# The squares of x added on VectorE, and the gate columns of group C brought forward in both layers

## The chip, the cores and the metric

The kernel runs on one core of one Trainium2 chip. The metric is the device time of one execution in microseconds. TensorE (PE) does the matrix multiplications, and its weight loads are listed apart as PEld; VectorE is DVE, ScalarE is ACT, GpSimd is POOL, and SyncE is SP, which here only issues transfers. Each engine executes its own queue in order and waits there for whatever its next instruction needs.

## The reference

Two layers work on 640 tokens of width 2048 (128 tokens of a prompt, 512 latent tokens). In each layer the normalised and modulated input goes through one combined projection, whose columns belong to three groups of heads; the three results go side by side through an output projection and are added to the input.

```python
shift, scale, gate = adaln(cvec, w_ada, b_ada)
h = rms_norm(x, norm_g) * (1.0 + scale) + shift
aq, ak, av, ag, bq, bff, bfb, bi, bg, cu, cv, cg = split_proj(h @ w_in)
q, k, v = qkv_heads(aq, ak, av, qg, kg, rope)
a_out = attend(q, k, v) * jax.nn.silu(ag)                       # A: attention, width 1024
b_out, s_f, s_b = hgrn_mixer(bq, bff, bfb, bi, bg, ...)          # B: gated recurrence, 4 heads, width 512
c_out = sgu_mixer(cu, cv, cg, lng, lnb, ws, bs)                  # C: cu * s(layer_norm(cv)) * silu(cg), width 512
y = jnp.concatenate([a_out, b_out, c_out], axis=-1) @ w_out
return x + gate * y, k, v, s_f, s_b
```

The modulation (shift, scale, gate) is a product of two vectors, one for prompt tokens and one for latent tokens, with a matrix of 2048 x 6144 per layer (w_ada).

## The kernel before, in words

*Projections.* The tokens lie as NT = 5 tiles of 128, the width as KT = 16 steps of 128. Each product in fp32 is made of three matmuls: weights are split into wh (ACT, L640) and wl (DVE, L641), activations into hh and hl, and hh·wh, hh·wl, hl·wh are summed. `rowmajor` gives 512 output columns with the tokens on the partitions: 240 matmuls (L652 to L654) into five PSUM banks "m". `colmajor` gives 128 output columns, columns on the partitions: 96 matmuls (L660) into two of those banks. There are five m banks in all, and three small ones, "s", for everything else.

*Work that rides along.* PE's long projections carry the rest of the layer in their gaps. A list `side` holds generators for the preparation of keys, the rotation of queries, the attention of one group and token tile (`attn`, whose rounds over key blocks end in the matmuls L953 to L955), the recurrence of a head (`hgrn`) and the mixing of group C (`sgu`). `tick` takes one step of the first of them, twice for each four steps of k in `colmajor` and about three times for each k in `rowmajor`; `flush` empties the list without further projection work in between. A second generator, the filler, computes the modulation that later stages need, in blocks of 512 columns: 16 steps, each of which loads 256 KB of w_ada and adds two products to a running sum on DVE (L302), then a step without work and one of closing matmuls on PE (L308 or L319). `fill` is called once at the end of each k group (15 times in a `rowmajor`, 4 times in a `colmajor`) and advances the filler by its rate: 1 in layer 0 (12 blocks, set before the projection AQ + 512) and 0.5 in layer 1 (4 blocks, set before AQ).

*Order.* The instructions of each engine are put in order by a scheduler when the kernel is built; what stands under `hi` goes ahead of other work that is ready. SP's queue issues nearly all loads of weights, in order; the ACT queue issues the small ones. Buffers come from pools: seven g of 128 x 640, five ev, five mg of 128 x 2560, four raw weights wr, three split weights, two for the filler's loads, and 16 each of hh and hl.

*Layer 0.* `setup` builds constants, among them the lower bounds of B's forget gates (L175 to L191). `first_round` loads x transposed, in four mg buffers; `first_norm` squares it on ACT, one k at a time, and sums over k and partitions with matmuls against a matrix of ones (L368), then takes the root (L370 to L372); then AK and the 128 columns of CU for head 0 are projected while the scale of the modulation comes in piece by piece (L240). `second_round` does AQ, `setup2` loads further constants, then come AQ + 512 and BI. CU 1 to 3 are projected and parked in DRAM (`cud`, by `cu_evac`), CU 0 is fetched back, multiplied by CG 0 and its SiLU, and parked again. Then come four heads of B with four `colmajor` each (BFF, BFB, BQ, BG), six of AG, the gates of A (`mul_evac`, whose last product POOL makes), a flush, CV with its layer norms, AG 6 and 7, a flush, in which `sgu` writes s into Cm. The four parked tiles are fetched and multiplied into Cm (L1354), then CG 1 to 3 are projected and multiplied into Cm as well, their last product on DVE. `split_mix` splits the 16 tiles of A, B and Cm into hh and hl (ACT, and L1229 on DVE or POOL), and `out_proj` multiplies by w_out in four `rowmajor`, whose results L1258 takes out of PSUM.

*Layer 1.* `begin_next` does the norm, AK, AQ, AQ + 512; then BI and the heads as above, seven AG, a flush, AG 7, CV, CU 0 and 1, a flush, CU 2 and 3 (multiplied into Cm straight from PSUM) and CG 0 to 3, all after the heads; `drain` finishes the filler, and the output projection writes the results.

The lines that say how a group is gated:

```python
s = self.ev() if gate else None
for hf, (o, n) in enumerate(HALF):                       # columns 0:384 and 384:640
    src = ps[hf][:, 0:n]
    if gate:
        nc.scalar.activation(s[:, o:o + n], src, AF.Exp, scale=-1.0)
    dv = dst[:, o // P:(o + n) // P, :]
    nc.vector.tensor_tensor(dv, dv, src.rearrange("p (t q) -> p t q", q=P), op=ALU.mult)   # L1208
if gate:
    self.sigma(s)                                        # min on DVE, Ln and Exp on ACT
    (eng or nc.gpsimd).tensor_tensor(dst, dst, s.rearrange(...), op=ALU.mult)              # L1211
```

Of the kernel before, what the change touches and what calls it, by code (L numbers as in the profile page):

```python
# [8 lines left out]
F32 = mybir.dt.float32  # L9
# [3 lines left out]
AF = mybir.ActivationFunctionType  # L13
ALU = mybir.AluOpType
# [4 lines left out]
P = 128  # L19
D = 2048  # L20
KT = D // P
# [3 lines left out]
NH = 4  # L25
# [3 lines left out]
HALF = ((0, 384), (384, 256))  # L29
AQ, AK, AV, AG = 0, 1024, 1280, 1536  # L30
BQ, BFF, BFB, BI, BG = 2560, 3072, 3584, 4096, 4608
CU, CV, CG = 5120, 5632, 6144
# [43 lines left out]
class Net:  # L76
# [57 lines left out]
    def setup(self):  # L134
        nc, I, C = self.nc, self.I, self.C
        cst = self.cst
        nc.scalar.preload_act_table_set("natural_log_exp_and_others")
        misc = cst.tile([P, 256], F32, name="misc")
        nc.sync.dma_start(misc, C["misc"])
        self.ident = misc[:, 0:128]  # L140
        self.m25 = misc[:, 192:217]
        self.dneg = misc[:, 224:244]
        self.sel = misc[:, 248:250]
        R = self.g(128)
        nc.scalar.dma_start(R[0:32], I["norm_g"].rearrange("l (a p) -> (l a) p", p=P))
        for l in range(2):
            nc.scalar.dma_start(R[32 + 32 * l:64 + 32 * l], I["b_ada"][l, 0:4096].rearrange("(a p) -> a p", p=P))
        nc.scalar.dma_start(R[96:112], I["hgrn_lb"].rearrange("l d (h p) -> (l d h) p", p=P))
        nc.scalar.dma_start(R[112:114], I["hgrn_norm_g"])
        CR = self.g(128)  # L150
        nc.sync.dma_start(CR[0:16], I["c_ctx"].rearrange("(a p) -> a p", p=P))
        nc.sync.dma_start(CR[16:32], I["c"][0].rearrange("(a p) -> a p", p=P))
        self.bias = cst.tile([P, 4], F32, name="bias")
        nc.vector.memset(self.bias[:, 0:1], EPS)
        nc.vector.memset(self.bias[:, 1:2], -0.5 * math.log(P))
        sg = self.g(128)
        nc.scalar.activation(sg[0:32], CR[0:32], AF.Exp, scale=-1.0)
        self.sigma(sg[0:32])
        nc.vector.tensor_tensor(sg[0:32], sg[0:32], CR[0:32], op=ALU.mult)
        self.sc = self.padded()  # L160
        self.shp = self.padded()
        self.s2 = cst.tile([P, KT, 2], F32, name="s2")
        self.ones = cst.tile([P, P], F32, name="ones")
        nc.vector.memset(self.ones, 1.0)
        b = self.bank()
        nc.tensor.transpose(b[:, 0:32], sg[0:32, :], self.ident[0:32, 0:32])
        for cd in range(2):
            nc.vector.tensor_copy(self.sc[:, :, cd], b[:, 16 * cd:16 * cd + 16])
            nc.vector.tensor_copy(self.s2[:, :, cd], b[:, 16 * cd:16 * cd + 16])
        b = self.bank()  # L170
        nc.tensor.transpose(b[:, 0:114], R[0:114, :], self.ident[0:114, 0:114])
        cols = cst.tile([P, 114], F32, name="cols")
        nc.vector.tensor_copy(cols, b[:, 0:114])
        self.cols = cols
        l0, l1 = cols[:, 96:104], cols[:, 104:112]  # L175
        lt = self.g(64).rearrange("p (a b) -> p a b", a=8)
        mx, e0, e1, sm_, p0, p1 = (lt[:, i] for i in range(6))
        nc.vector.tensor_tensor(mx, l0, l1, op=ALU.max)
        nc.vector.tensor_tensor(e0, l0, mx, op=ALU.subtract)
        nc.vector.tensor_tensor(e1, l1, mx, op=ALU.subtract)  # L180
        nc.scalar.activation(lt[:, 1:3], lt[:, 1:3], AF.Exp)
        nc.vector.tensor_tensor(sm_, e0, e1, op=ALU.add)
        nc.vector.reciprocal(sm_, sm_)
        nc.vector.tensor_tensor(p0, e0, sm_, op=ALU.mult)
        nc.vector.tensor_tensor(p1, e1, sm_, op=ALU.mult)
        self.lb = cst.tile([P, 2, 8], F32, name="lb")
        self.oml = cst.tile([P, 2, 8], F32, name="oml")
        nc.vector.tensor_tensor(self.lb[:, 0], p0, p0, op=ALU.subtract)
        nc.vector.tensor_tensor(self.lb[:, 1], p0, p1, op=ALU.add)
        nc.vector.tensor_tensor(self.lb[:, 1], self.lb[:, 1], p0, op=ALU.subtract)  # L190
        nc.vector.tensor_scalar(self.oml, self.lb, -1.0, 1.0, op0=ALU.mult, op1=ALU.add)  # L191
        self.gs = cst.tile([P, 2, KT, 2], F32, name="gs")
        self.sh = cst.tile([P, 2, KT, 2], F32, name="sh")

    def setup2(self):
        nc, I, C = self.nc, self.I, self.C
        cst = self.cst
        self.rope = cst.tile([P, 2, 4, 64], F32, name="rope")
        nc.scalar.dma_start(self.rope, C["rope"])
        self.scan_f = cst.tile([P, T], BF16, name="scan")  # L200
# [159 lines left out]
    def first_norm(self, xm):  # L360

        nc = self.nc
        b = [self.bank(), self.bank()]
        for k in range(KT):
            s = self.g()
            nc.scalar.activation(s, xm[k // 4][:, k % 4], AF.Square)
            for hf, (o, n) in enumerate(HALF):
                nc.tensor.matmul(b[hf][:, 0:n], lhsT=self.ones, rhs=s[:, o:o + n], start=k == 0, stop=k == KT - 1)  # L368
        r = self.g()
        for hf, (o, n) in enumerate(HALF):  # L370
            nc.scalar.activation(r[:, o:o + n], b[hf][:, 0:n], AF.Ln, bias=self.bias[:, 0:1], scale=1.0 / D)
        last = nc.scalar.activation(r, r, AF.Exp, scale=-0.5)  # L372
        return r, last.ins
# [938 lines left out]
    def layer(self, l):  # L1312
        W = self.I["w_in"][l]
        nc = self.nc
        self.hh, self.hl = [], []
        self.A, self.rq = {}, {}
        if l == 0:
            self.begin(W)
        else:
            self.begin_next(l, W)  # L1320
        self.side.append(self.q_rope(1))
        self.side += [self.attn(l, 1, t) for t in range(NT)]
        self.bi_evac(self.rowmajor(W, BI))
        if l == 0:
            for h in range(1, 4):
                self.cu_evac(h, self.colmajor(W, CU + h * P))
            u = self.g()
            nc.scalar.dma_start(u, self.cud[0])
            self.mul_evac(self.colmajor(W, CG), u.rearrange("p (t q) -> p t q", q=P), True, nc.vector)
            nc.scalar.dma_start(self.cud[0], u)  # L1330
        for h in range(NH):
            es = [self.z_evac(self.colmajor(W, c0 + h * P)) for c0 in (BFF, BFB)]
            q = self.q_gate(self.colmajor(W, BQ + h * P))
            if h == 0:
                self.flush()
            self.b_gate(l, h, self.colmajor(W, BG + h * P))
            self.side.append(self.hgrn(l, h, es, q))
        early = 6 if l == 0 else 7
        for h in range(early):
            self.mul_evac(self.colmajor(W, AG + h * P), self.av_view(h), True)  # L1340
        self.flush()
        if l > 0:
            self.mul_evac(self.colmajor(W, AG + 7 * P), self.av_view(7), True)
        self.sgu_evac(self.rowmajor(W, CV))
        self.side.append(self.sgu(l))
        if l == 0:
            ps = [self.colmajor(W, AG + h * P) for h in (6, 7)]
            self.flush()
            for h in (6, 7):
                self.mul_evac(ps[h - 6], self.av_view(h), True)  # L1350
            for h in range(4):
                u = self.g()
                nc.scalar.dma_start(u, self.cud[h])
                nc.vector.tensor_tensor(self.Cm[:, h], self.Cm[:, h], u, op=ALU.mult)  # L1354
        else:
            ps = [self.colmajor(W, CU + h * P) for h in range(2)]
            self.flush()
            for h in range(4):
                self.mul_evac(ps[h] if h < 2 else self.colmajor(W, CU + h * P), self.view(self.Cm, h), False)
        for h in range(1 - min(l, 1), 4):  # L1360
            self.mul_evac(self.colmajor(W, CG + h * P), self.view(self.Cm, h), True, nc.vector)
        if l > 0:
            self.drain()
        self.split_mix()
        self.out_proj(l)
        self.drain()

    def cu_evac(self, h, ps):
        nc = self.nc
        u = self.g()  # L1370
        with self.hi():
            nc.scalar.activation(u[:, 0:384], ps[0][:, 0:384], AF.Copy)
            nc.vector.tensor_copy(u[:, 384:640], ps[1][:, 0:256])
        nc.scalar.dma_start(self.cud[h], u)

    def run(self):
# [47 lines left out]
```

## Time and profile before

| what | value |
|---|---|
| median of three runs | 2344.2 us (2340.97 to 2345.61) |
| the profiled execution's own time | 2338.18 us |
| its span from the first to the last instruction | 2336.4 us |
| mean granted TensorE clock in it | 0.988 |
| busy: PE, PEld, DVE, ACT, POOL | 2261.4, 1968.0, 1424.3, 778.7, 293.9 us |
| read from and written to HBM | 280.38 and 13.73 MB, 126 GB/s over the span |

A row of a view by groups names the line, the engine, the operation, the output and the inputs by their pool names with shape and count, then busy time and mean; after a bar stands the idle time of the engine just before these instructions and what ended it. A row of the timeline has the start, the length, and in square brackets the wait just before. In a chain of waits, "PE s L1143 <- DVE g L1137: 7.0, 2, 6.1" says that PE's instruction at L1143 waited for DVE's at L1137, 7.0 us in all, twice, 6.1 us the longest. A row of the windows gives from and to, the length, the busy time and the number of instructions of PE, PEld, DVE, ACT and POOL, the granted clock (1.00 is full speed), the busy share of the DMA engines and what they moved in GB/s; where one line of one engine was asked for, its busy time alone stands in place of the five.

### The profile page before, as it was taken

The numbers are of one execution on the slowest core, as the hardware profiler recorded it, in microseconds if no ns is written. First come the engines' busy times: TensorE is split into PE (matmuls) and PEld (weight loads), VectorE is DVE, ScalarE is ACT, GpSimd is POOL, SyncE is SP. The second block draws the span as 40 slices with busy tenths as digits, with TensorE's granted clock in tenths as the row PEclk, the third lists the DMA queues.
The fourth block names the chain that finished last, engine by engine and source line by source line (L and its number), as shares of the span: only waits on it lengthen the run. The fifth ranks groups of instructions, "written<-read, shape, count | busy, mean of one in ns | idle before, by whom it ended". The sixth has DMA issues, their size and how long they took to land.

```text
span 2336.4 us, 34944 instructions
## 1 busy us (share of the span) xinstructions
PE 2261.4 (97%) x13308; PEld 1968.0 (84%) x13308; DVE 1424.3 (61%) x2612; ACT 778.7 (33%) x1605; POOL 293.9 (13%) x234
## 2 busy tenths in 40 slices
PE   7999999999999989989999999999999999999999
PEld 5766678899999888977787878799999998998887
DVE  3436987768887766666667455855875942434223
ACT  3323434343334322332224234344343332223111
POOL 0000111002122211011112010101222220101110
PEclk9999999999999999999999999999999999999999
DMA  9675632434433354355552221322332323324332
GB/s 321 218 254 191 209 117 83 148 95 120 126 117 104 111 163 144 111 192 171 173 170 91 77 68 47 115 68 72 111 94 76 114 90 92 103 75 149 106 106 84
DMA packets 264876, 296.41 MB, mean 127 GB/s; under 512 B 17378, under 2 KB 166772, under 8 KB 262916
## 3 DMA queue, kind: packets, MB, share of 16 engines
q1 hardware_dynamic: 254368, 271.27, 37.2%
q10 hardware_dynamic: 10340, 22.91, 3.2%
q8 instruction: 104, 1.70, 0.3%
q14 instruction: 64, 0.52, 0.1%
HBM read 280.38 MB, written 13.73 MB: 126 GB/s over the span
## 4 chain that ended last, share of the span: by engine, by line
PE 75%; DVE 12%; DMA 7%; issue 2%; ACT 1%; POOL 0%; DVEq 0%; ACTq 0%; POOLq 0%
PE m L660 29%; PE m L652 11%; PE m L653 11%; PE m L654 11%; DMA wa<-in_w_ada_dram 6%; DVE aacc L302 4%; DVE wl L641 2%; PE s L240 2%; PE s L895 1%; PE s L941 1%; PE s L1105 1%; PE s L1072 1%; PE s L953 1%; PE s L954 1%; PE s L319 1%
## 5 line engine op out<-in xcount | busy, mean ns | idle before, releaser
L641 DVE TENSOR_TENSOR wl<-wr,wh 128x512 fp32r<-128x512 f32 (+1 forms) x535 | 401.5, 752 | 575.2 <-ACT wh L640 566.7
L640 ACT ACTIVATE wh<-wr 128x512 fp32r<-128x512 f32 (+1 forms) x535 | 336.1, 629 | 971.0 <-PE m L654 557.2
L652 PE MATMUL m<-wh,hh 128*128 128x512 f32 x1440 | 571.6, 397 | 9.2 <-DVE mg L1208 5.3
L653 PE MATMUL m<-wl,hh 128*128 128x512 f32 x1440 | 568.5, 395 | 3.5 <-DVE wl L641 3.5
L654 PE MATMUL m<-wh,hl 128*128 128x512 f32 x1440 | 565.6, 393 | 0.0
L660 PE MATMUL m<-hh,wh 128*128 128x384 f32 x2016 | 478.1, 317 | 0.0
L660 PE MATMUL m<-hl,wh 128*128 128x384 f32 x2016 | 465.0, 311 | 0.0
L660 PE MATMUL m<-hh,wl 128*128 128x384 f32 x2016 | 464.6, 311 | 0.0
L302 DVE SCALAR_TENSOR_TENSOR aacc<-wa,s,aacc 128x512 f32<-128x512 f32 x480 | 368.6, 801 | 72.9 <-DMA wa<-in_w_ada_dram 72.3
L652 PEld LDWEIGHTS m<-wh,hh 128*128 128x128 f32 x1440 | 272.0, 189 | 84.5 <-issue 10.3
L653 PEld LDWEIGHTS m<-wl,hh 128*128 128x128 f32 x1440 | 272.7, 189 | 64.2 <-DVE wl L641 7.4
L654 PEld LDWEIGHTS m<-wh,hl 128*128 128x128 f32 x1440 | 272.4, 189 | 59.0 <-issue 2.6
L660 PEld LDWEIGHTS m<-hh,wh 128*128 128x128 f32 x2016 | 312.5, 190 | 9.8 <-issue 8.1
L660 PEld LDWEIGHTS m<-hl,wh 128*128 128x128 f32 x2016 | 311.5, 189 | 0.4
L660 PEld LDWEIGHTS m<-hh,wl 128*128 128x128 f32 x2016 | 311.1, 189 | 0.3
L1090 POOL TENSOR_TENSOR mg<-ev,Dt 128x512 f32<-128x512 f32 x80 | 95.7, 1213 | 321.5 <-PE s L1105 107.2
L1260 POOL TENSOR_TENSOR mg<-mg,ev 128x512 f32<-128x512 f32 x30 | 43.9, 1473 | 287.9 <-DVE ev L1258 287.1
L751 POOL TENSOR_TENSOR mg<-g,g 128x256 f32<-128x256 f32 x32 | 32.8, 1047 | 263.8 <-DVE g L749 145.5
L925 ACT ACTIVATE g<-g,st,qs 128x384 f32<-128x384 f32 (+1 forms) x64 | 48.1, 752 | 36.0 <-DVE st L921 36.0
L228 ACT ACTIVATE ev<-ev 128x640 f32<-128x640 f32 x40 | 29.5, 738 | 72.3 <-DVE ev L227 71.2
L945 DVE TENSOR_TENSOR g<-s,g 128x512 fp32r<-128x512 f32 x56 | 38.4, 687 | 24.0 <-ACT g L944 18.1
L1045 POOL TENSOR_TENSOR g<-g,EG 128x512 f32<-128x512 f32 x16 | 22.7, 1416 | 239.4 <-DVE Dt L1030 125.1
(272 smaller groups left out, 1984.6 us busy)
## 6 DMA issues: line engine op xcount, KB each, us to landing
wr<-in_w_in_dram SPq DMA_DIRECT2D x406, 256.0 KB, 2.9
wa<-in_w_ada_dram SPq DMA_DIRECT2D x278, 256.0 KB, 3.0
wr<-in_w_out_dram SPq DMA_DIRECT2D x128, 256.0 KB, 2.9
wa<-in_w_ada_dram SPq DMA_DIRECT2D x16, 1024.0 KB, 6.7
wa<-in_w_in_dram SPq DMA_DIRECT2D x9, 1024.0 KB, 6.5
wa<-in_w_ada_dram SPq DMA_DIRECT2D x44, 128.0 KB, 3.3
mg<-const_xT_dram SPq DMA_DIRECT2D x4, 1280.0 KB, 5.8
x<-mg SPq DMA_DIRECT2D x20, 256.0 KB, 2.1
```

What stands on the lines that cost most here:

```text
L240: return self.nc.tensor.matmul(acc[32 * q:32 * q + 32, 0:n], lhsT=lhs[:, kk, :], rhs=rhs, start=kk < 4, stop=kk >= 12, skip_group_check=True)
L302: nc.vector.scalar_tensor_tensor(acc[:, cd], r, sc, acc[:, cd], op0=ALU.mult, op1=ALU.add)
L640: nc.scalar.activation(wh, raw, AF.Copy)
L641: nc.vector.tensor_tensor(wl, raw, wh.bitcast(F32), op=ALU.subtract)
L652: nc.tensor.matmul(ps, lhsT=hh, rhs=wh[:, 0], start=k == 0, stop=False)
L653: nc.tensor.matmul(ps, lhsT=hh, rhs=wl[:, 0], start=False, stop=False)
L654: nc.tensor.matmul(ps, lhsT=hl, rhs=wh[:, 0], start=False, stop=k == KT - 1)
L660: self.nc.tensor.matmul(ps[hf][:, 0:n], lhsT=w[:, a], rhs=h[:, o:o + n], start=k == 0 and i == 0, stop=k == KT - 1 and i == 2)
L925: nc.scalar.activation(dst[h], src[h], AF.Exp, bias=nmx[:, h:h + 1], scale=rq[:, h:h + 1], accum_out=den[:, h:h + 1])
L945: nc.vector.tensor_tensor(pt[1], pb, pt[0].bitcast(F32), op=ALU.subtract)
L1090: nc.gpsimd.tensor_tensor(k.rearrange("p (i c s) -> p i c s", i=4, c=4), bc(c4(pre[d][0])[:, j], 1, 4), bc(dd, 3, 32), op=ALU.mult)
L1260: (nc.vector if c == 3 else nc.gpsimd).tensor_tensor(xs, xs, y, op=ALU.add)
```

## The change

`first_norm` adds the sixteen squares on DVE into one tile (`tot`) and multiplies that by the ones: 15 additions and 2 matmul instructions in place of 32. The code of the lower bounds goes from `setup` to `setup2`; what it computes is the same. `cgate` takes the place of `cu_evac`: for each of the four heads it projects CU, evacuates it to a g buffer u, projects CG directly behind it, multiplies u by CG and its SiLU (last product on DVE) and parks u in DRAM. It runs for all four heads after BI, in both layers; in layer 0 the CU of head 0 still comes from the first round. The stages behind the heads are then the same in both layers: AG 0 to 5, flush, CV, AG 6 and 7, flush, the gating of AG 6 and 7 with its last product on DVE, the four parked tiles fetched and multiplied into Cm, `split_mix`, output projection. No projection stands between that gating and `split_mix` any more.

```diff
@@ setup -> setup2
+    def setup2(self):
+        nc, I, C = self.nc, self.I, self.C
+        cst = self.cst
+        l0, l1 = self.cols[:, 96:104], self.cols[:, 104:112]
         lt = self.g(64).rearrange("p (a b) -> p a b", a=8)
...
         nc.vector.tensor_scalar(self.oml, self.lb, -1.0, 1.0, op0=ALU.mult, op1=ALU.add)
-    def setup2(self):
...
         self.rope = cst.tile([P, 2, 4, 64], F32, name="rope")
         nc.scalar.dma_start(self.rope, C["rope"])
@@ first_norm
+        tot = self.g()
         for k in range(KT):
-            s = self.g()
+            s = self.g() if k else tot
             nc.scalar.activation(s, xm[k // 4][:, k % 4], AF.Square)
-            for hf, (o, n) in enumerate(HALF):
-                nc.tensor.matmul(b[hf][:, 0:n], lhsT=self.ones, rhs=s[:, o:o + n], start=k == 0, stop=k == KT - 1)
+            if k:
+                nc.vector.tensor_tensor(tot, tot, s, op=ALU.add)
+        for hf, (o, n) in enumerate(HALF):
+            nc.tensor.matmul(b[hf][:, 0:n], lhsT=self.ones, rhs=tot[:, o:o + n], start=True, stop=True)
@@ layer
         self.bi_evac(self.rowmajor(W, BI))
-        if l == 0:
-            for h in range(1, 4):
-                self.cu_evac(h, self.colmajor(W, CU + h * P))
-            u = self.g()
-            nc.scalar.dma_start(u, self.cud[0])
-            self.mul_evac(self.colmajor(W, CG), u.rearrange("p (t q) -> p t q", q=P), True, nc.vector)
-            nc.scalar.dma_start(self.cud[0], u)
+        for h in range(NH):
+            self.cgate(l, h, W)
         for h in range(NH):
...
-        early = 6 if l == 0 else 7
-        for h in range(early):
+        for h in range(6):
             self.mul_evac(self.colmajor(W, AG + h * P), self.av_view(h), True)
         self.flush()
-        if l > 0:
-            self.mul_evac(self.colmajor(W, AG + 7 * P), self.av_view(7), True)
         self.sgu_evac(self.rowmajor(W, CV))
         self.side.append(self.sgu(l))
-        if l == 0:
-            ps = [self.colmajor(W, AG + h * P) for h in (6, 7)]
-            self.flush()
-            for h in (6, 7):
-                self.mul_evac(ps[h - 6], self.av_view(h), True)
-            for h in range(4):
-                u = self.g()
-                nc.scalar.dma_start(u, self.cud[h])
-                nc.vector.tensor_tensor(self.Cm[:, h], self.Cm[:, h], u, op=ALU.mult)
-        else:
-            ps = [self.colmajor(W, CU + h * P) for h in range(2)]
-            self.flush()
-            for h in range(4):
-                self.mul_evac(ps[h] if h < 2 else self.colmajor(W, CU + h * P), self.view(self.Cm, h), False)
-        for h in range(1 - min(l, 1), 4):
-            self.mul_evac(self.colmajor(W, CG + h * P), self.view(self.Cm, h), True, nc.vector)
+        ps = [self.colmajor(W, AG + h * P) for h in (6, 7)]
+        self.flush()
+        for h in (6, 7):
+            self.mul_evac(ps[h - 6], self.av_view(h), True, nc.vector)
+        for h in range(NH):
+            u = self.g()
+            nc.scalar.dma_start(u, self.cud[h])
+            nc.vector.tensor_tensor(self.Cm[:, h], self.Cm[:, h], u, op=ALU.mult)
@@ cu_evac -> cgate
-    def cu_evac(self, h, ps):
+    def cgate(self, l, h, W):
         nc = self.nc
         u = self.g()
-        with self.hi():
-            nc.scalar.activation(u[:, 0:384], ps[0][:, 0:384], AF.Copy)
-            nc.vector.tensor_copy(u[:, 384:640], ps[1][:, 0:256])
+        if l == 0 and h == 0:
+            nc.scalar.dma_start(u, self.cud[0])
+        else:
+            ps = self.colmajor(W, CU + h * P)
+            with self.hi():
+                nc.scalar.activation(u[:, 0:384], ps[0][:, 0:384], AF.Copy)
+                nc.vector.tensor_copy(u[:, 384:640], ps[1][:, 0:256])
+        self.mul_evac(self.colmajor(W, CG + h * P), u.rearrange("p (t q) -> p t q", q=P), True, nc.vector)
         nc.scalar.dma_start(self.cud[h], u)
```

More of the change, by code (lines that the diff above doesn't have):

```diff
@@ L174, in setup @@
         self.cols = cols
-        l0, l1 = cols[:, 96:104], cols[:, 104:112]
+        self.gs = cst.tile([P, 2, KT, 2], F32, name="gs")
+        self.sh = cst.tile([P, 2, KT, 2], F32, name="sh")
+    def setup2(self):
+        nc, I, C = self.nc, self.I, self.C
+        cst = self.cst
+        l0, l1 = self.cols[:, 96:104], self.cols[:, 104:112]
         lt = self.g(64).rearrange("p (a b) -> p a b", a=8)
@@ L191, in setup @@
         nc.vector.tensor_scalar(self.oml, self.lb, -1.0, 1.0, op0=ALU.mult, op1=ALU.add)
-        self.gs = cst.tile([P, 2, KT, 2], F32, name="gs")
-        self.sh = cst.tile([P, 2, KT, 2], F32, name="sh")
-    def setup2(self):
-        nc, I, C = self.nc, self.I, self.C
-        cst = self.cst
         self.rope = cst.tile([P, 2, 4, 64], F32, name="rope")
```

## The prediction, on record before the change was run

> **What bounds the kernel now.** I read the profile page first: its span, the busy times and the chain of work that ended last.
>
> ```profile
> span 2336.4 us, 34944 instructions
> PE 2261.4 (97%) x13308; PEld 1968.0 (84%) x13308; DVE 1424.3 (61%) x2612; ACT 778.7 (33%) x1605; POOL 293.9 (13%) x234
> PE 75%; DVE 12%; DMA 7%; issue 2%; ACT 1%; POOL 0%; DVEq 0%; ACTq 0%; POOLq 0%
> ```
>
> TensorE (PE) carries three quarters of the chain, VectorE (DVE) and DMA a fifth. The change leaves the number of projection matmuls as it is, so a gain must come from places where PE waits or runs at a lower clock. The windows by stage show which places those are (columns: length, then busy time of PE, PEld, DVE, ACT, POOL, granted clock, DMA share, GB/s).
>
> ```profile
> 25.00:50.00 25.00, 22.75 (x141) 15.84 (x140) 8.83 (x17) 8.63 (x18) 0.00 (x0) 0.93 0.96 321
> 50.00:75.00 25.00, 24.29 (x134) 15.39 (x133) 14.85 (x23) 8.44 (x17) 0.00 (x0) 1.00 0.99 339
> 757.00:857.00 100.00, 88.78 (x645) 85.57 (x645) 78.57 (x136) 30.83 (x68) 21.96 (x16) 0.95 0.46 139
> 913.00:955.00 42.00, 36.55 (x239) 36.09 (x239) 34.71 (x56) 10.27 (x24) 10.00 (x7) 0.92 0.48 146
> 955.00:999.00 44.00, 44.00 (x306) 44.00 (x305) 28.05 (x45) 17.86 (x31) 8.67 (x3) 1.00 0.39 118
> 999.00:1063.00 64.00, 57.67 (x253) 47.19 (x253) 41.88 (x62) 17.65 (x30) 6.04 (x4) 0.95 0.57 191
> 1823.00:1926.00 103.00, 98.22 (x721) 94.94 (x720) 66.45 (x118) 35.08 (x75) 21.57 (x16) 0.98 0.35 104
> 1926.00:2114.00 188.00, 188.00 (x1160) 177.47 (x1159) 73.13 (x115) 53.79 (x96) 16.08 (x11) 1.00 0.32 95
> ```
>
> In order these are: two pieces of the opening, where the DMA engines are full; AG 0 to 5 of layer 0; its AG 6 and 7; its CG 1 to 3, with PE never idle; the first quarter of its output projection; AG 0 to 5 of layer 1; and AG 6 to CG 3 of layer 1, without an idle moment. PE's waits in those windows, and the pieces of the chain in front of two of them:
>
> ```profile
> PE s L1143 <- DVE g L1137: 7.0, 2, 6.1
> PE s L1072 <- ACT g L1068: 4.1, 1, 4.1
> PE s L1193 <- DVE mg L1194: 5.1, 1, 5.1
> PE m L652 <- DVE mg L1208: 5.3, 1, 5.3
> PE s L1072 <- ACT g L1068: 3.6, 1, 3.6
> ...
> 831.03 4.05 DMA wa<-in_w_ada_dram
> 836.62 4.14 DMA wa<-in_w_ada_dram
> 1834.61 3.24 DMA wa<-in_w_ada_dram
> 1839.39 2.74 DMA wa<-in_w_ada_dram
> ```
>
> The first two waits are of 757 to 857, then one each of 913 to 955, 999 to 1063 and 1823 to 1926. DVE executes in order; its filler (the modulation sums, L302) sits in its queue waiting for a weight load, and the instruction that PE needs stands behind. These waits, not DVE's 61%, are the prize.
>
> **The change part by part.** First, where the filler runs. One block of it is 18 steps, and its sums bunch up behind the block before:
>
> ```profile
> 814.00:862.00 48.00, 22.69 (x30) 0.93 0.57 175
> 862.00:891.00 29.00, 0.00 (x0) 1.00 0.32 90
> 1800.00:1863.00 63.00, 24.12 (x30) 0.97 0.39 117
> 1863.00:1951.00 88.00, 0.00 (x0) 1.00 0.28 82
> ```
>
> These are DVE's L302 alone. All four large waits above lie inside such a bunch or just behind it. A projection of 128 columns calls the filler 4 times, one of 512 columns 15 times, at rate 1 in layer 0 and 0.5 in layer 1, so a block ends at calls 126, 144, 162 in layer 0 and at 108 and 144 in layer 1. Counted from the code, layer 0 has 30 calls by the end of BI; three more column projections before the heads move every later head 12 calls on. Call 126 now falls in AG 3 and call 144 in CV; after the change they fall at the end of AG 0 and in AG 5. In layer 1 eight projections more, 32 calls: call 108 moves from the last gate of head 3 to that of head 1, call 144 from CV to AG 0. The last bunch, behind call 108, is then over before AG 0.
>
> - Layer 1, AG 0 to 5: no L302 left there. The wait of 3.6 goes, and with it the clock lost (0.02 of 103 us, 2 us) and about 1 us of small waits: -6.5, between -7 and 0 (0 if another bunch lands on a head's step). What is late next is the hgrn chain itself, which PE hides outside the bunches.
> - Layer 0, AG 0 to 5: two bunches, 7.0 + 4.1 us of waits and 0.05 x 100 = 5 us of clock, together 16. After the change one bunch starts at the end of AG 0 and the next only in AG 5. The wait of 6.1 sits 34 us behind the start of its bunch; after, the same step comes some 10 us behind one. I take a third: -5, between -16 and +3.
> - Layer 0, AG 6 and 7 (5.1 us of waits, 0.08 x 42 = 3.4 us of clock): call 162 puts a pause of the filler at the SGU's layer norms. I take -2, between -8 and +3.
> - Layer 0, hand-over to the output projection. The cover of 955 to 999 goes: split_mix, whose buffers come free only as the last projection passes, now follows AG 7. The filler is at the same call as before, so the wait of 5.3 for L1208 stays. DVE gets the last multiplication of AG 6 and 7 (from POOL) on top, and the splits shift against the SGU's adds:
>
> ```profile
> L1211 DVE TENSOR_TENSOR mg<-mg,ev 128x640 f32<-128x640 f32 x7 | 5.7, 820 | 3.3 <-ACT ev L229 3.3
> L1354 DVE TENSOR_TENSOR mg<-mg,g x4: 814/818/819, 939.3 to 949.7; 128x640 f32<-128x640 f32 x4
> ```
>
>   Two of 0.82, and up to four products of 0.82 (L1354) that cannot hide: +3, between -3 and +8.
> - Layer 1, the same hand-over, with no filler: DVE is 39% busy in 1926 to 2114, PE waits for the evacuation of AG 7 alone. +1, between 0 and +4. Without that slack it would cost what layer 0 pays, up to 8.
> - Parking: four stores and four loads more in layer 1, none in layer 0 beyond moved ones, at a DMA share of 0.3; nothing on SP's queue, the ACT queue issues them. Nothing, but each u holds one of the seven g buffers from CU's evacuation until CG's product is stored, beside the attention, which already waits for them:
>
> ```profile
> L945 DVE TENSOR_TENSOR g<-s,g 128x512 fp32r<-128x512 f32 x56 | 38.4, 687 | 24.0 <-ACT g L944 18.1 <-PE s L954 5.8
> 367.00:533.00 166.00, 9.72 (x21) 3.95 (x21) 0.99 0.35 106
> 1531.00:1604.00 73.00, 4.60 (x10) 1.89 (x10) 1.00 0.21 60
> ```
>
>   In the last two rows, of L953 alone, there is one a round: 21 + 10 rounds beside the parked columns. At worst each waits a whole L945 more, 31 x 0.687 = 21 us; the projection matmuls between two rounds hide most. I take +2.5 (0.08 a round), between 0 and +21.
>
> Now the opening.
>
> ```profile
> 7.29 1.31 SPq L407 DMA_DIRECT2D mg<-const_xT_dram  x3
> 11.96 19.26 PE L368 MATMUL s<-g,ones 128*128 128x384 f32 x64 [1.72 <-DVE g L184]
> 31.80 0.74 ACT L372 ACTIVATE g<-g 128x640 f32<-128x640 f32 x1
> 35.94 0.73 PE L652 MATMUL m<-wh,hh 128*128 128x512 f32 x1 [1.44 <-ACT hh L382]
> 61.58 0.33 SPq L423 DMA_DIRECT2D mg<-in_w_ada_dram  x1
> mg<-in_w_ada_dram SPq DMA_DIRECT2D x1, 256.0 KB, 5.4
> 67.83 0.64 PE L240 MATMUL s<-mg,pad 128*32 128x512 f32 x4
> ```
>
> The 64 matmul records (19.26 us) become 15 adds at 0.82 (the row of L1354), 12.3 us on an idle DVE, and 4 records. The last of x arrives about 19 us in (three loads of 1.31 MB from 7.29 on take some 12 us at the 321 to 339 GB/s of the first two windows), four adds follow, then matmuls and the two Ln and Exp: the row's scale is ready near 26 instead of 32.5. The first projection matmul then starts near 30, 5.9 us earlier. But the DMA engines are full (shares 0.96 and 0.99 above), so loads land when they did: the one issued at 61.58 takes 5.4, lands at 66.98, and its matmuls start at 67.83. Only 0.85 us of the lead gets through, unless SP's queue issues that load earlier. I take 0, between -5.9 and +1.7 (below).
>
> The lower-bound arithmetic (L175 to L191) moves from setup to setup2, where PE already waits for a load that the ACT queue issues:
>
> ```profile
> 216.22 0.41 PE L738 MATMUL s<-misc,g 128*128 128x128 f32 x2 [1.97 <-DMA g<-in_cache_k_dram]
> 217.34 0.63 PE L653 MATMUL m<-wl,hh 128*128 128x512 f32 x1
> 220.58 0.39 PE L652 MATMUL m<-wh,hh 128*128 128x512 f32 x1
> 11.06 0.21 ACT L181 ACTIVATE g<-g 128x16 f32<-128x16 f32 x1 [1.89 <-DVE g L180]
> ```
>
> L181 waited 1.89 us on DVE; in setup2 the loads of the masks and of the cached keys stand behind it on the ACT queue, and PE's matmuls of L738 behind those. The cost is between 0 and +2 (one such wait); I take 0, since DVE has little else queued at that point.
>
> A lead that meets a late load becomes a wait of some 5 us, and behind the 1.97 us wait above matmuls took 0.63 instead of 0.39 each: a wait costs clock too. I estimate 8 matmuls of 0.2 more, up to 1.7 us. The Trainium skill (TensorE: Matmul & The Clock Gate, Part 1) says that the clock halves after an idle window of about 3.4 us and returns after as long a busy one. By that rule the opening would end 0.9 us slower (1.7 less 0.85), the sum would be -6 instead of -7, and the short wait at 216 should have cost nothing; the trace differs on that.
>
> The sum: 0 + 0 - 6.5 - 5 - 2 + 3 + 1 + 2.5 = -7.0 us. The profiled execution took 2338.18 us, its span 2336.4; it lies 6.0 under the median of the three runs, 2344.2. Taken off the median: 2337.2.
>
> **The rivals.** *The opening's lead passes whole.* If SP's queue takes the mg loads of the scale as soon as their buffer is free (about 54 us in), they land in time and all 5.9 us arrive. For it: PE has next to no waits from 64 to 200. Against: in the trace that load stands behind three others although its buffer was free. -7 - 5.9: 2331.
>
> *The gains cancel.* The bunch behind call 126 hits AG 2's transposes as the old one did, and the hand-over in layer 0 costs its upper end: 0 for AG, +8: -7 + 5 + 5 = +3, so 2347.
>
> *The attention runs out of buffers* (slower). With u resident, a round's two tiles must wait for the round before. For it: L945 already waits 5.8 us on L954 with seven. Against: two of the rounds' tiles are freed within the same round. At a whole L945 a round: -9.5 + 21 = +12, so 2356. It decides for slower above (9.5 + 4.7) / 31 = 0.46 us a round.
>
> **How the numbers follow.** About 0.2% (4.7 us) is what a measurement here can tell from none. The forecast (between -12 and -2) 0.42, the whole lead 0.20, cancelling 0.20, buffers 0.18. Faster by over 0.2%: 0.36 of the forecast's and all of the lead's, 0.56; within: the rest and cancelling, 0.26; slower: 0.18. The range from 2327 to 2350 leaves out most of the buffer case and the deepest leads; the forecast alone lies in 2332 to 2342.
>
> **What would show it.** L302 absent from layer 1's AG stage and no wait of L1072 there; in layer 0 a bunch starting at AG 0's end and the wait of L1143 under 3 us; L368 down to 4 records near 24 us, and either a wait of PE for mg near 62 us or everything behind 5.9 us earlier; a wait for L1208 at the start of layer 0's output projection of 5 to 13 us; L945's waits on L954 unchanged. Wrong would make it: bunches that land on other heads' steps (L1067, L1072), since only their calls, not their effect on each head, are counted here, or a new order of the instructions.

## The result, and the profile after

The changed kernel took 2330.9 us (median of four runs, 2330.1 to 2331.7) against 2342.6 us before (four runs, 2340.5 to 2345.6): a ratio of 0.9949, 95% interval 0.9932 to 0.9966, or 11.7 us less. Its profiled execution took 2331.7 us; the page begins:

```profile
span 2329.9 us, 34862 instructions
PE 2240.3 (96%) x13248; PEld 1953.3 (84%) x13248; DVE 1428.7 (61%) x2631; ACT 781.5 (34%) x1609; POOL 288.9 (12%) x230
PE 76%; DVE 11%; DMA 6%; issue 2%; ACT 1%; POOL 0%; DVEq 0%; SPq 0%; ACTq 0%; POOLq 0%
```

Nothing here tells where the time went: the shares are those of before. The stages do. Each length in the table runs from the first projection matmul of one stage to that of the next, in the two profiled executions; layer 1 begins where the last projection matmul of layer 0 ends. (AQ's times, here and below, are those of a matmul near AK's end; AQ's own first one comes 1.5 us later in each execution, which leaves the differences as they are.) Three projections of 128 columns at 14.08 us moved from behind CV to ahead of the heads; their 42.2 us are taken out of the third row of "after" and put into the fourth.

| stage | before | after | difference |
|---|---|---|---|
| start to AQ | 128.8 | 127.5 | -1.3 |
| AQ to the end of BI, layer 0 | 238.0 | 237.5 | -0.5 |
| its columns up to CV | 490.2 | 498.5 | +8.3 |
| CV to its output projection | 141.9 | 136.0 | -5.9 |
| its output projection | 237.6 | 230.8 | -6.9 |
| layer 1 to the end of BI | 295.1 | 295.2 | +0.1 |
| its columns and CV | 582.3 | 582.1 | -0.3 |
| its output projection | 222.4 | 222.4 | 0.0 |

The sum is -6.5, the difference of the spans. The other 5 us lie in the runs of before: 17 later ones spread from 2337.5 to 2347.8, and the one that was profiled (2338.2) is near their fast end. In a trace of the old order that took 2341.8 (the first experiment) the same waits behind the filler are longer, 7.9 instead of 6.1 for L1143 and 4.8 instead of 4.1 for L1072.

So the largest gain sits where a loss of 3 us was forecast. And the columns up to CV, where a gain was forecast, lost 8.3 us: AG 0 to 5 gained 8.6 (the second rows below), while the columns and heads ahead of AG, where 2.5 us were forecast for buffers alone, lost 16.8. Lines from the end of `first_norm` to `out_proj` have numbers three higher in the changed kernel (L1105 is L1108, L1208 is L1211), and one more in the paced one. Below stand the rows from PE's waits in the changed kernel's whole execution on which this rests, and stages of the two kernels by windows, before first and after behind it (from and to, length, busy time of PE, PEld, DVE, ACT and POOL, clock, DMA share, GB/s):

```profile
PE s L1108 <- DVE mg L1081: 24.7, 5, 7.1
PE s L1196 <- DVE mg L1197: 3.5, 2, 2.6
PE s L1075 <- ACT g L1071: 2.2, 2, 1.5
PE s L1146 <- DVE g L1140: 1.1, 2, 0.5
PE m L655 <- DVE mg L1211: 0.6, 1, 0.6
```

```profile
457.46:739.64 282.18, 279.62 (x2063) 267.57 (x2062) 218.33 (x397) 107.76 (x233) 51.32 (x39) 0.99 0.38 113
739.64:857.04 117.40, 106.18 (x782) 102.58 (x780) 95.89 (x169) 40.05 (x94) 25.00 (x18) 0.96 0.45 135
```

```profile
513.95:796.95 283.00, 267.14 (x1960) 259.25 (x1959) 210.33 (x365) 95.05 (x203) 52.01 (x39) 0.96 0.41 119
796.95:905.77 108.82, 103.79 (x798) 100.45 (x796) 82.49 (x152) 39.51 (x94) 27.49 (x18) 1.00 0.42 124
```

The second row of each is AG 0 to 5 of layer 0, the first its heads. (By these starts the prediction's windows 757 to 857 and 1823 to 1926 begin with AG 1, not AG 0.) The AG stage became 8.6 us shorter and got its clock back (0.96 to 1.00), as forecast. The heads took as long as before although PE was busy 12.5 us less in them (some of the attention had already run beside the added columns): PE stood idle for 15.9 instead of 2.6 us, and the clock fell from 0.99 to 0.96. A wait that was in no list before, PE's L1108 for L1081, holds 24.7 us. The timelines around its longest case, VectorE first, then TensorE (start, length, engine, line, operation, operands, count, wait):

```profile
612.51 3.65 DVE L302 SCALAR_TENSOR_TENSOR aacc<-wa,s,aacc 128x512 f32<-128x512 f32 x3
616.09 0.68 DVE L644 TENSOR_TENSOR wl<-wr,wh 128x512 fp32r<-128x512 f32 x1
616.98 1.42 DVE L302 SCALAR_TENSOR_TENSOR aacc<-wa,s,aacc 128x512 f32<-128x512 f32 x2 [0.21 <-DMA wa<-in_w_ada_dram]
618.31 0.34 DVE L1081 SCALAR_TENSOR_TENSOR mg<-mg,EG,s 128x128 f32<-128x128 f32 x1
619.25 0.75 DVE L302 SCALAR_TENSOR_TENSOR aacc<-wa,s,aacc 128x512 f32<-128x512 f32 x1 [0.60 <-DMA wa<-in_w_ada_dram]
619.92 0.34 DVE L1081 SCALAR_TENSOR_TENSOR mg<-mg,EG,s 128x128 f32<-128x128 f32 x1
620.18 0.74 DVE L302 SCALAR_TENSOR_TENSOR aacc<-wa,s,aacc 128x512 f32<-128x512 f32 x1
620.84 0.34 DVE L1081 SCALAR_TENSOR_TENSOR mg<-mg,EG,s 128x128 f32<-128x128 f32 x1
```

```profile
613.73 0.46 PE L663 MATMUL m<-hh,wl 128*128 128x384 f32 x2
621.33 1.08 PE L1108 MATMUL s<-mg,g 128*32 128x128 f32 x16 [7.14 <-DVE mg L1081]
623.58 0.74 PE L663 MATMUL m<-hh,wl 128*128 128x384 f32 x2
626.99 0.68 PE L663 MATMUL m<-hh,wl 128*128 128x384 f32 x2
628.09 0.46 PE L663 MATMUL m<-hh,wl 128*128 128x384 f32 x2
```

L1081 reads the states' update out of one of the three s banks and so frees it for PE's L1108. Its three instructions of 0.34 us stand among the filler's sums, and PE, in order, holds a projection back for 7 us. The same happened in the projections of three heads of layer 0 (7.1, 4.8 and 3.5 us), once in its AG (2.2) and once in layer 1 (7.1).

### The profile page after: what moved, and what is told of

Same layout as the page of the kernel before. It is cut to its first block, busy times and chain, and to the rows that moved or that the text cites. A ratio compares the mean times of both kernels' runs of the same rounds, so it can differ in the third digit from the quotient of the medians.

```text
span 2329.9 us, 34862 instructions
## 1 busy us (share of the span) xinstructions
PE 2240.3 (96%) x13248; PEld 1953.3 (84%) x13248; DVE 1428.7 (61%) x2631; ACT 781.5 (34%) x1609; POOL 288.9 (12%) x230
## 4 chain that ended last, share of the span: by engine, by line
PE 76%; DVE 11%; DMA 6%; issue 2%; ACT 1%; POOL 0%; DVEq 0%; SPq 0%; ACTq 0%; POOLq 0%
PE m L663 31%; PE m L655 11%; PE m L656 11%; PE m L657 11%; DMA wa<-in_w_ada_dram 5%; DVE aacc L302 4%; DVE wl L644 2%; PE s L898 2%; PE s L240 1%; PE s L944 1%; PE s L1108 1%; PE s L956 1%; PE s L957 1%; PE s L1123 1%; PE s L958 1%
## 5 line engine op out<-in xcount | busy, mean ns | idle before, releaser
L644 DVE TENSOR_TENSOR wl<-wr,wh 128x512 fp32r<-128x512 f32 (+1 forms) x535 | 393.7, 737 | 569.7 <-ACT wh L643 564.3
L948 DVE TENSOR_TENSOR g<-s,g 128x512 fp32r<-128x512 f32 x56 | 38.5, 688 | 23.5 <-ACT g L947 16.7
L947 ACT ACTIVATE g<-s 128x512 fp32r<-128x512 f32 x56 | 32.6, 596 | 56.6 <-PE s L944 50.0
L1108 PE MATMUL s<-mg,g 128*32 128x128 f32 x640 | 27.6, 293 | 24.7 <-DVE mg L1081 24.7
```

Of the source, the lines that this page charges most:

```text
L644: nc.vector.tensor_tensor(wl, raw, wh.bitcast(F32), op=ALU.subtract)
L1108: nc.tensor.matmul(ab[32 * i:32 * i + 32, 0:P], lhsT=qe[:, n * P + 32 * i:n * P + 32 * i + 32], rhs=K[d][:, ri * P:(ri + 1) * P], start=Tr ...
```

## The experiments

The theory (A): what the order of the columns changed is which steps stand behind the filler's sums on VectorE, and nothing else of size. Rivals: the opening carries the gain (B), layer 1 gained (C), the order is shorter in itself (S), the new waits come from the order or the parked buffers and not from the filler (D).

**The opening alone.** The kernel before with the new `first_norm` and the lower bounds in `setup2`.

> The kernel before with only the two edits of the opening (squares summed on VectorE, lower bounds in setup2). Theory A (the lead is cut by late loads): the first projection matmul starts 2.9 us earlier, at 33.1, but AQ begins only some 1.3 us earlier (127.6 instead of 128.8), and the whole run ends 1 to 2 us earlier, all else being the same instructions: 2341 against 2342.6. Rival B (the opening carries most of the measured 11.7 us, which the profiled executions do not show): 2333 to 2337.

2342.3 us against 2342.1: ratio 1.0002 (0.9991 to 1.0012). The first projection matmul starts at 32.7, AQ at 127.7. B falls; the 1 to 2 us that A expected were not seen, but a gain of up to 2 us lies inside the interval.

**The order alone.** The changed kernel with `first_norm` and `setup` of before.

> The changed kernel with the opening of before. Theory A: 1 to 2 us over the changed kernel, about 2332.5, with the same waits behind the heads (L1105 for L1078, some 25 us in all). Rival B: most of the gain gone, 2338 or more.

2334.2 us, 0.9961 (0.9949 to 0.9973): the order brings some 8 us without the opening, so B falls here too (A had expected 2332.5). PE waits 22.5 us for L1078 in its trace, and the output projection of layer 0 takes 229.5 us. AQ begins at 129.0.

**Layer 0 alone.** The changed kernel with the old order in layer 1:

```diff
-        for h in range(NH):
-            self.cgate(l, h, W)
+        if l == 0:
+            (new order, to the loads of cud)
+        else:
+            (old order)
```

> The changed kernel with layer 1 in its old order. Theory A (layer 1 won nothing: its wait of 3.8 us for L1068 went and one of 7.1 for L1078 came): within 1 us of the changed kernel, 2330 to 2332, the span of layer 1 from the end of BI to the output projection 582 as in both. Rival C (layer 1 gains the 6.5 us of the forecast in undisturbed runs): 2336 to 2338.

2332.1 us, 0.9962 (0.9948 to 0.9975); its layer 1 took 584.0 us for columns and CV (582.1 in the changed kernel), with 3.9 us of waiting for ACT in front of L1075. In the profiled execution layer 1 thus exchanged one wait for another, and C is not borne out; but two of the six runs took 2337 and 2341 us, and the interval reaches to 2336, so C is not excluded by the times alone.

**The sums left out**, in both kernels:

```diff
-                else:
+                elif k == KT - 1:
                     nc.vector.scalar_tensor_tensor(acc[:, cd], r, sc, acc[:, cd], ...)
```

> The kernel before with 14 of each 16 steps of the filler's sums left out (only the first and the last step add to the sum; all its loads stay), so the modulation it computes is not the reference's. Theory A (what the change moves is where these sums delay the recurrence and the evacuations): from the first column projection to the output projection layer 0 takes 595 to 610 instead of 632, its output projection 224 to 228 instead of 237.6, because the wait for L1208 at its start goes; layer 1 from its column projections on 572 to 577 instead of 582; in all 2285 to 2305.

> The changed kernel with the same 14 of 16 steps left out. Theory A: the long waits for L1081 go as well, and it comes out at the kernel before without these sums less the 1 to 2 us of the opening: the two within 3 us of each other, and their output projections of layer 0 within 2 us. Rival S (the new order is shorter in itself: no CG columns between sgu and the splits, fewer products on Cm): 7 to 11 us faster than the kernel before without the sums, most of it in the output projection of layer 0.

2281.1 us (before, 2278.8 to 2281.8) and 2281.3 us (changed, 2278.6 to 2289.0): ratios 0.9737 (0.9723 to 0.9751) and 0.9748 (0.9727 to 0.9769). Without the sums the two kernels take the same time within the intervals, and each is faster, by 62 and 50 us, the first by more than A had expected. S falls. By stages, layer 0 from its first column to its output projection takes 583.1 and 582.5, layer 1's columns and CV 570.5 in both. The output projection of layer 0 takes 222.1 and 227.5: here the new order is 5.4 us longer, against the 2 us that A allowed. In the two profiled executions this is made up elsewhere: the changed kernel is 2.9 us ahead at its first column projection, and its layer 1 up to the end of BI is 3.3 us shorter. There the code is the same, and so is the wait in front of L941 or L944 (3.1 and 3.2 us near 1337), but behind it the clock is 0.50 from 1335.4 to 1342.2 in the kernel before and 1.00 in the changed one. In the changed one's output projection a weight split is late:

```profile
991.49 0.80 PE L655 MATMUL m<-wh,hh 128*128 128x512 f32 x1 [3.06 <-ACT wh L643]
990.81 1.25 ACT L643 ACTIVATE wh<-wr 128x512 fp32r<-128x512 f32 x2 [8.25 <-DMA wr<-in_w_out_dram]
```

The loads of w_out stand between 1 MB loads of x that the projection's end needs (three of the four are issued behind its start at 960.2, from 971.0 to 983.7; in the old order two are, behind 963.7). That these loads delay the split is read off the trace, not tested. The loss is of about the size that the prediction had looked for at the hand-over, but not of its kind: the prediction had VectorE's products and splits there, here PE waits for a weight.

**The filler started later**, by 8 calls in layer 0 and 10 in layer 1:

```diff
         self.fill_rate = 1.0
+        self.credit = -8.0
...
         self.fill_rate = 0.5
+        self.credit = -5.0
```

> The changed kernel with the filler started 8 calls later in layer 0 and 10 calls later in layer 1 (its credit begins at -8 and -5), nothing else: its blocks then begin 6, 8, 10 and 12 calls into a head of 16 in layer 0 and 9 in layer 1, where no long wait was seen, instead of 14, 0, 2, 4 and 15. Theory A (the time follows from which step of the recurrence lies behind the sums on VectorE): PE's waits at the third matmul group of a head for an s bank (24.7 us in the changed kernel) fall under 8, heads and AG of layer 0 take about 370 us instead of 391.8, those of layer 1 about 356 instead of 364; in all 20 to 30 us less, 2300 to 2311. Rival D (the new waits come from the order of the columns or from parked buffers, not from the filler): within 4 us of 2331.

2326.1 us, 0.9931 (0.9919 to 0.9943), 5 less than the changed kernel and far from 2300. The waits for L1081 did fall to 3.0 us in all, but others came: 8.9 us at L1131 for L1111, 6.9 us at L1146 for L1140. Heads and AG of layer 0 took 389.8 instead of 391.8 us. The columns ahead of the heads became 8.4 us shorter, but from the start of the output projection's last product to the first projection of layer 1 it took 74.7 instead of 65.8 us; there the later filler's sums still stand among the evacuations on VectorE; layer 1, where a step comes at every second call, 576.9 instead of 582.1 for columns and CV. The expectation assumed that some places in a head are free; in layer 0 a block lasts 18 calls and a head 16, so some step of the recurrence always stands behind the sums. D falls with it (the waits went as the filler moved), but A's number was wrong.

**The sums paced.** Each step's two sums are queued on VectorE behind the weight split that precedes their call, instead of as early as their load allows:

```diff
+        self.pace = nc.vector.tensor_tensor(wl, raw, wh.bitcast(F32), op=ALU.subtract).ins     # wsplit
...
+            with self.tc.issue_after(self.pace):                                               # ada_steps
                 for cd in range(2):
                     ...                                                                        # the two sums
```

> The changed kernel with each of the filler's sums queued on VectorE behind the weight split that precedes its call, so that a block's sums follow the pace of the projections instead of running ahead of it. Theory A: in layer 1 (one step for two calls) two sums no longer stand behind each other, the wait of 7.1 us for L1081 falls under 3 and heads and AG take 357 instead of 364; in layer 0 (one step a call) the waits shrink by a third; 2318 to 2326. Rival D (the waits are not the filler's): 2329 to 2333.

2302.5 us, 0.9830 (0.9816 to 0.9844), 28 us less than the changed kernel and more than expected; once more, on another chip, 2303.6 (0.9842, 0.9828 to 0.9855):

> The paced changed kernel once more, beside the one above on the same chip: 2301 to 2304.5.

It beats both kernels. Of its waits these two stand in place of the 24.7 and 3.5 us above:

```profile
PE s L1109 <- DVE mg L1082: 3.7, 1, 3.7
PE s L1197 <- DVE mg L1198: 2.8, 1, 2.8
```

Layer 0 takes 617.2 instead of 634.4 us from its columns to its output projection, and 223.5 instead of 230.8 for that; layer 1's columns and CV 571.1, within a microsecond of the kernel without sums.

**The kernel before, paced, and the new order with the old opening, paced.**

> The kernel before with the filler's sums queued behind the weight splits, as in the paced version of the changed kernel (2302.5 us). Theory A (the gain of the change lay in where the filler's sums fell): paced, the two orders come within 4 us of each other, 2300 to 2307, and the wait of 5.3 us for L1208 at the start of layer 0's output projection is under 1.5. Rival S (the new order keeps a gain of its own): 2309 to 2315.

> The new order of the columns with the opening of before, and the filler's sums queued behind the weight splits. Paced, the kernel before took 2309.2 and the changed one 2302.5; the profiled executions put 2.4 us of this on the opening and no more than 1.3 on any later stage. Theory O (the difference that is left is the opening's): 2304 to 2306 here, 2 to 4 us over the paced changed kernel beside it. Rival S (the order of the columns keeps a gain of its own when paced): within 1.5 us of the paced changed kernel.

2309.2 us (0.9862, 0.9846 to 0.9879) and 2306.8 us (0.9851, 0.9837 to 0.9864). Paced, the order is worth 2.4 us (between two chips) and the opening 3.2 (2306.8 against 2303.6 beside it), neither clear of its interval; together 5.6 to 6.7. That is over the 4 us that A allowed, at the lower edge of S; O holds in the difference, 0.8 us above its range of times. Of the 8 us that the order brings in the kernel as it is, about 2 are thus left when the sums are paced; the rest goes with where the sums fall, as A has it. Pacing alone took 34 us off the kernel before. The wait of 5.3 us for L1208 is 1.5 us in the paced kernel before, about as A expected.

**AG 7 behind the flush.** Why did that wait go in the changed kernel, which is not paced? One idea was that AG 6 and 7 are now evacuated under cover of `sgu`.

```diff
-        ps = [self.colmajor(W, AG + h * P) for h in (6, 7)]
+        ps = [self.colmajor(W, AG + 6 * P)]
         self.flush()
+        ps.append(self.colmajor(W, AG + 7 * P))
```

> The changed kernel with AG 7 projected behind the flush of sgu instead of ahead of it. Theory H (the output projection of layer 0 became 7 us shorter because the results of AG 6 and 7 are evacuated while PE works off sgu, so that no evacuation stands behind the filler's sums when it starts): a wait of 3 to 6 us for L1211 comes back at its start, the output projection takes 235 to 239 instead of 230.8 and the run 2335 to 2340. Rival I (it became shorter because DVE has fewer products and splits to do at that time): 2329 to 2333, no such wait.

2335.6 us, 0.9971 (0.9962 to 0.9981), in the range of H, but not by its mechanism: PE waited 1.2 us for L1211, and the output projection took 232.4. H falls; I has the wait right and the time wrong. What the traces of before and after show in VectorE's queue at that point:

```profile
998.94 4.04 DVE L302 SCALAR_TENSOR_TENSOR aacc<-wa,s,aacc 128x512 f32<-128x512 f32 x4
1006.30 1.41 DVE L302 SCALAR_TENSOR_TENSOR aacc<-wa,s,aacc 128x512 f32<-128x512 f32 x2 [3.32 <-DMA wa<-in_w_ada_dram]
1007.63 0.88 DVE L1208 TENSOR_TENSOR mg<-mg,m 128x384 f32<-128x384 f32 x2
```

```profile
999.69 2.07 DVE L302 SCALAR_TENSOR_TENSOR aacc<-wa,s,aacc 128x512 f32<-128x512 f32 x3
1001.67 0.88 DVE L1211 TENSOR_TENSOR mg<-mg,m 128x384 f32<-128x384 f32 x2
```

Before, six sums and a load that was 3.3 us late stood ahead of the evacuation that frees PE's banks; after, three sums whose loads were there. Why the scheduler's order put fewer there was not settled.

**Fewer additions in the opening.** On the paced kernel, only the odd squares are added on VectorE, the even ones go to TensorE as before:

```diff
-            if k:
+            if k > 1 and k % 2:
                 nc.vector.tensor_tensor(tot, tot, s, op=ALU.add)
+            if k % 2 == 0 or k == KT - 1:
+                (two matmuls against the ones, of s or of tot)
```

> The paced version of the changed kernel with only the odd squares of x added on VectorE (7 additions) and the even ones sent to TensorE as before. The row's scale is then ready about 3 us earlier, near 25 us, and AK starts near 30 instead of 32.2. Theory L (the lead of the opening is cut by loads that land when they did): AQ begins within 0.8 us of the 126.4 us of the paced version, and the time stays within 1.5 us of 2302.5. Rival M (the lead of the first edit was small only because 15 additions took 13.7 us; what is gained on top of it arrives): AQ at 123.5 to 124.5, 2299 to 2300.

2304.1 us (0.9837, 0.9822 to 0.9852), beside 2302.5 and 2303.6. AK began at 31.1 (expected near 30), AQ at 127.2, 0.8 us later than without the edit, and the time is 1.6 us from 2302.5, a tenth more than L allowed. PE reached the group of loads that the prediction had pointed at, 0.8 us before one of them landed:

```profile
64.33 2.98 PE L240 MATMUL s<-mg,pad 128*32 128x512 f32 x8 [0.81 <-DMA mg<-in_w_ada_dram]
```

M falls, and L holds as far as so small a lead can show it: an AK that starts 1.1 us earlier bought nothing behind that load.

## Why the prediction was right, and where it was not

The time forecast from the profiled execution, -7.0 us, was -6.5 there and -11.7 in the medians, inside the range. But that is luck: it came out through terms that were wrong and cancelled. The terms for the stages that the prediction looked at (AG in both layers, AG 6 and 7) had the right sign and roughly the right size; the columns and heads ahead of AG, priced at 2.5 us for buffers alone, cost 16.8 us in layer 0 and 6.2 in layer 1, and the hand-over in layer 0 came out with the wrong sign.

- *Opening: 0, measured -1.3.* The step was right: of the lead, only what the loads leave got through. The lead at the first matmul was 2.9 us instead of 5.9, in part because the 15 additions were busy for 13.7 us from 10.27 on, not 12.3, and ended at 24.5, behind the last square (21.5):

```profile
10.27 2.67 DVE L369 TENSOR_TENSOR g<-g,g 128x640 f32<-128x640 f32 x3
13.44 11.04 DVE L369 TENSOR_TENSOR g<-g,g 128x640 f32<-128x640 f32 x12 [0.49 <-ACT g L367]
33.08 0.50 PE L655 MATMUL m<-wh,hh 128*128 128x512 f32 x1 [1.44 <-ACT hh L385]
65.52 2.09 PE L240 MATMUL s<-mg,pad 128*32 128x512 f32 x8
```

  Each addition ran 0.82 us, as priced, but the twelve in a row began 0.93 us apart; the row's scale was ready at 28.3 instead of near 26. Of the 2.3 us of lead left at 65.52 (67.83 before), the group's 2.09 instead of 1.06 us took one. What got through is the 0.85 us of the prediction and the 0.45 us by which the load that it named was issued earlier (61.13 for 61.58). Over all profiled executions, AQ begins at 126.4 to 127.7 in the nine with the new opening or its variant and at 128.4 to 129.8 in the five with the old one. The rival of the whole lead, -13 in all, gave the time most nearly (2331) and is not what happened.
- *Setup2: 0.* Measured: the wait for the cached keys is 2.2 instead of 2.0 us, AQ to BI 153.6 in both.
- *Layer 1, AG: -6.5, measured -5.3 for AG 0 to 5 but -0.3 for columns and CV as a whole.* The calls were counted rightly: the block ended at 1773.7 in the last gate of head 1, AG is free of sums but for the last block's closing, the wait for L1068 is gone, and AG 0 to 5 took 101.6 instead of 106.9 us. The failed step is "what is late next": the sums behind that block fell on the recurrence that runs beside head 2's projections and cost a wait of 7.1 us at L1108; columns and heads together became 6.2 us longer.
- *Layer 0, AG 0 to 5: -5, measured -8.6 for AG and a net +8.3 up to CV.* The same step: the block at AG 0's end came as forecast (L1146 0.5 us; PE idle for 5.0 us in AG instead of 11.2), but the three blocks before it, each moved by 12 calls onto other steps of the heads, were never priced, and columns and heads together became 16.8 us longer. The prediction named this as what could undo it.
- *AG 6 and 7: -2, measured -2.3.* They took 39.3 instead of 41.6 us, waited 3.5 us instead of 5.1, and the clock was 1.00 instead of 0.92. The other 3.6 of the 5.9 us from CV on had no term: CV became 1.8 us shorter, and CG 1 to 3 had taken 44.0 us there, not 42.2.
- *Hand-over in layer 0: +3, measured -6.9.* The step "the filler is at the same call as before, so the wait of 5.3 for L1208 stays" failed. It took the call of the program for the place in VectorE's queue: the wait fell to 0.6 us, and the first of the four products took 57.2 instead of 65.1 us. With the sums gone, the new order is 5.4 us longer there, the sign of the forecast, but by a late weight load and not by the products and splits that it named.
- *Hand-over in layer 1: +1, and buffers: +2.5; measured nothing of either.* L948 waits 23.5 us in all where L945 waited 24.0, and without the sums the stages with the parked columns are equal to 0.6 us.

## What to carry to other kernels

When background work on an in-order engine runs as early as its data allow, a new order of the main work changes mostly which instruction is caught behind it; price every place where the background work now falls, not only the one from which it moves away. If a wait moves from place to place as the order changes, take away its cause: tying the background steps to the pace of the main work brought 28 us here, on top of 11.7 from the new order and opening, and 34 us without these two. And price an order with the background work left out as well: one pair of kernels showed that the new order and opening were then worth no more than the few microseconds that such runs can tell.

## What the runs showed of the hardware

A wait costs more than its length. Behind the wait of 7.14 us at 621.33 pairs of projection matmuls took 0.74 instead of 0.46 us until about 627; behind the 3.06 us at 991.49 the next ones took 0.63 instead of 0.40 us for about 3 us. The Trainium skill (TensorE: Matmul & The Clock Gate, Part 1) puts the fall of the clock behind an idle window of about 3.4 us and its return behind as long a busy one. The return came 3.1 and 6.1 us behind the end of the two waits, one to two times that, but the fall did not need so long a wait: 2.0 us (at 216.22 in the kernel before) and 3.1 us were enough. The granted clock is 0.50 for 10.2 us around the wait at 621.33 (617.2 to 627.5) and for 3.4 us at the one at 991.49 (991.2 to 994.6). A short wait does not always cost clock: behind 2.2 us at 863.48 in the changed kernel, and behind 3.2 us at 1337.33 in that kernel without the sums, it stayed at 1.00. Of PE's waits of 3.5 us or more, all 38 that end later than 100 us in the fourteen executions had a stretch at 0.50 that began during the wait or within 3.5 us of its end, 3.4 to 13.7 us long.
